# Reordering how an attention pair's q and k leave PSUM

## The chip, the cores and the metric

The kernel runs on one core of one Trainium2 chip. The metric is the device time of one execution in microseconds (us). The core has five engines that matter here: TensorE (PE, matrix multiplication; PEld is its weight load), ScalarE (ACT), VectorE (DVE), GpSimd (POOL) and SyncE (SP), which only issues DMAs. Each engine works through its own list of instructions in order and waits at an instruction until what it needs is there. TensorE writes its results into PSUM, eight banks of 128 partitions by 512 float32.

## The reference

Three transformer layers over 512 tokens of width 1024, float32. The first layer mixes block-sparse attention (8 heads of 64) with gated linear attention; the other two mix causal attention with a forget bias (8 heads of 64) with retention. Every layer ends in a feed-forward block of width 4096. What matters here is the attention, which the kernel computes for two heads at a time:

```python
scores = jnp.einsum('bqhd,bkhd->bhqk', q_i, k_i).astype(jnp.float32) * scale
logits = jnp.where(causal, scores + bias, -jnp.inf)
p = jax.nn.softmax(logits, axis=-1)
return jnp.einsum('bhqk,bkhd->bqhd', p.astype(v.dtype), v)
```

## The kernel before

`block1` is the first layer, `block2` runs twice. All large products are split into a high and a low part (`fp32r` tiles with names ending in h and l), three matmuls for each product. PSUM is two pools of four banks: `mm` for projections, `at` for attention and everything else that is short.

The order of work on TensorE is written out at build time by a planner, the class `Weave`. Each piece of the model is a generator; the planner keeps its own clock, books assumed costs on ScalarE, VectorE and GpSimd (`Engine`: ScalarE 0.2 + 0.83 per 1000 columns, VectorE 0.17 + 1.04, GpSimd 0.25 + 2.1), and resumes a generator when its event is due, the one with the lower priority number first. `wv.fork()` starts a new chain of bookings at the planner's present time, `wv.done()` gives an event that is due 0.6 (`LAG`) after the latest booking since the generator was resumed. A generator that yields `(1, ev)` asks for one free `at` bank and the event. The planner keeps an account of the `at` banks and none of the `mm` banks. The other engines' lists are ordered by a list scheduler in the framework: by program order, but an instruction that the scheduler believes ready may pass one that it believes is not. The framework adds the waits.

`attention_pair(i, ...)` handles heads 2i and 2i+1; there are four pairs in each of the three layers. It is given two PSUM banks, q and k, with head 0 on partitions 0 to 63 and head 1 on partitions 64 to 127. Its first loop makes three tiles for each head: `qs` (128 partitions: on the head's own half r the rounded q, on the other half x what rounding left), `kh` and `kl` (the high and the low part of k, each on both halves). In order, for each head:

- ScalarE writes `qs[r]` from the q bank; VectorE writes `qs[x]` from the q bank and `qs[r]`
- ScalarE writes `kh[r]` from the k bank; VectorE writes `kl[r]` from the k bank and `kh[r]` (`split2`)
- ScalarE copies `kh[r]` to `kh[x]`, then `kl[r]` to `kl[x]`
- `bias(2 * i + hh)` loads the head's bias row with a DMA on SyncE: `row` from `cd` in block2, where GpSimd then adds the causal mask (`cm`), or `g` from `revp` in block1

After that come the scores (TensorE, `at<-kh,qs` and `at<-kl,qs`), the masked minimum and the softmax (VectorE and ScalarE: `ea`, `eb`, `ec`, `mx`), transposes, copies (`pta`, `ptb`, `ptc`) and the product with v.

In block2 the q and k banks come from `proj_a`, so they are two of the four `mm` banks; pairs follow each other, and behind pair 3 stands `proj_b` for the retention values, which takes all four `mm` banks, one for each of four token tiles t = 0 to 3: t = 2 is given the bank of pair 3's q, t = 3 that of its k. In block1 transposes put q and k into two `at` banks.

Of the kernel before, what the change touches and what calls it, by code (L numbers as in the profile page):

```python
# [10 lines left out]
F32 = mybir.dt.float32  # L11
F32R = mybir.dt.float32r
I32 = mybir.dt.int32
AF = mybir.ActivationFunctionType
ALU = mybir.AluOpType
# [252 lines left out]
def model_kernel(ctx: ExitStack, tc: tile.TileContext, I, out):  # L268
# [13 lines left out]
    wv = Weave(8 - NM)  # L282
    act, dve, pool = Engine(nc.scalar, wv, 0.2, 0.83), Engine(nc.vector, wv, 0.17, 1.04), Engine(nc.gpsimd, wv, 0.25, 2.1)
    uid = [0]

    def nm(s):
        uid[0] += 1
        return f"{s}_{uid[0]}"

    def bt(s="b", dt=F32):  # L290
        return pb.tile([P, T], dt, tag="b", name=nm(s))
# [4 lines left out]
    def vt(s="v", w=16):  # L296
        if w > 16:
            return pv.tile([P, 40], F32, tag="w", name=nm(s), bufs=5)
        return pv.tile([P, 16], F32, tag="v", name=nm(s))
# [4 lines left out]
    def at_ps():  # L304
        t = psa.tile([P, T], F32, tag="at", name=nm("at"))
        wv.bank(t)
        return t

    def mm(out, lhsT, rhs, start, stop, more=False):

        nc.tensor.matmul(out, lhsT, rhs, start=start, stop=stop, skip_group_check=more)  # L311
        n = rhs.free_size()
        if lhsT.dtype == F32:
            c = max(4 * n, 1024 if n < P else 0) * (0.5 if lhsT.free_size() <= 64 else 1.0)
        else:
            c = n if n >= 256 else 4 * n
        wv.now += c / 2400.0

    def transpose(out, in_):
        nc.tensor.transpose(out, in_, ident)  # L320
        wv.now += 0.11

    def copy(o, i):
        act.activation(o, i, AF.Copy)

    def sub_lo(o, x, hi, eng=dve):
        eng.tensor_tensor(o, x, hi.bitcast(F32), ALU.subtract)

    def split2(hi, lo, x, scale=None):

        if scale is None:
            copy(hi, x)
            sub_lo(lo, x, hi)
        else:
            act.activation(hi, x, AF.Copy if isinstance(scale, float) else AF.Identity, scale=scale)
            dve.scalar_tensor_tensor(lo, x, scale, hi.bitcast(F32), ALU.mult, ALU.subtract)
# [170 lines left out]
    def attention_pair(i, operands, v, bias, acts_out, done=None):  # L507

        qps, kps, qscale, kscale = yield from operands()
        room, ops = [], []
        for hh in range(2):
            wv.fork()
            r, x = slice(64 * hh, 64 * hh + 64), slice(64 - 64 * hh, 128 - 64 * hh)
            sc = lambda c: c if c is None or isinstance(c, float) else c[r]
            qs, kh, klo = bt("qs", F32R), bt("kh", F32R), bt("kl", F32R)
            act.activation(qs[r], qps[r], AF.Copy if isinstance(qscale, float) else AF.Identity, scale=sc(qscale))
            dve.scalar_tensor_tensor(qs[x], qps[r], sc(qscale), qs[r].bitcast(F32), ALU.mult, ALU.subtract)  # L520
            split2(kh[r], klo[r], kps[r], sc(kscale))
            copy(kh[x], kh[r].bitcast(F32))
            copy(klo[x], klo[r].bitcast(F32))
            ops.append((qs, kh, klo, bias(2 * i + hh), wv.done()))
        ec, pc2 = bt("ec"), bt("ptc")
        for hh in range(2):
            qs, kh, kl, pieces, ev = ops[hh]

            ea, eb = bt("ea"), bt("eb")
            es = [eb[:, 384:512], ec[:, 256 * hh : 256 * hh + 256], eb[:, 0:384], ea]  # L530
            for t in (3, 2, 1, 0):
                if t:
                    yield 1, ev
                    sx = at_ps()
                    for u in (t, 0) if t == 1 else (t,):
                        m = max(P * u + P, 256)
                        s = sx[:, 256 * u : 256 * u + 256] if t == 1 else sx
                        mm(s[:, :m], qs[:, u * P : u * P + P], kh[:, :m], True, False)
                        mm(s[:, :m], qs[:, u * P : u * P + P], kl[:, :m], False, True)
                s = sx[:, 256 * t :] if t < 2 else sx  # L540
                wv.fork()
                e = es[t]
                mx = 3.0e38
                c = vt("mx")
                for j, (a, b, tl) in enumerate(pieces(t)):
                    dve.tensor_tensor_reduce(e[:, a:b], s[:, a:b], tl, 1.0, mx, ALU.add, ALU.min, c[:, j : j + 1])
                    mx = c[:, j : j + 1]
                act.activation(e, e, AF.Exp, bias=mx, scale=-1.0, accum_out=c[:, 2:3])
                dve.reciprocal(c[:, 3:4], c[:, 2:3])
                dve.tensor_scalar(e, e, c[:, 3:4], None, ALU.mult)  # L550
                if t == 3:
                    ev3 = wv.done()
            ev = wv.done()
            ev.t = max(ev.t, ev3.t)
            room.append((es, ev))

        pts = []
        for hh in range(2):
            es, t0 = room[hh]
            pta, ptb = bt("pta"), bt("ptb")  # L560
            pt = [pta, ptb[:, 0:384], pc2[:, 256 * hh : 256 * hh + 256], ptb[:, 384:512]]
            for ks, dst in (((0,), pta), ((1, 3), ptb), ((2,), pt[2])):
                yield 1, t0
                tp = at_ps()
                n = 0
                for kt in ks:
                    for t in range(kt, NT):
                        transpose(tp[:, n : n + P], es[t][:, kt * P : kt * P + P])
                        n += P
                if hh:  # L570
                    copy(dst, tp[:, 0:n])
                else:
                    dve.tensor_copy(dst, tp[:, 0:n])
            pts.append(pt)
        yield (1,)
        y = at_ps()
        for kt in range(NT):
            for hh in range(2):
                h = 2 * i + hh
                mm(  # L580
                    y[64 * hh : 64 * hh + 64, kt * P : T],
                    v[kt][:, 64 * h : 64 * h + 64],
                    pts[hh][kt],
                    kt == 0,
                    kt == NT - 1,
                )
        acts_out.split(i, y)
        if done is not None:
            wv.mark(done)
# [43 lines left out]
    class Quarter:  # L633
# [16 lines left out]
        def pieces(self, i, j):  # L650

            for k in range(2):
                k0 = self.k0 + 512 * i + 256 * k
                off, size = offs[(self.name, self.l, k0, k0 + 256, 512 * j, 512 * j + 512, "")]
                src = I["wall"][off : off + size].rearrange("(p w) -> p w", p=P)
                for c in range(2):
                    yield src[:, 512 * c : 512 * c + 512]
# [408 lines left out]
    def block1():  # L1066
# [32 lines left out]
        for i in range(4):  # L1099
            wv.spawn(attention_pair(i, operands(i), mv, moba_bias, ym, adone[i]), 1)  # L1100
# [160 lines left out]
    def block2(l, xw, h):  # L1261
# [11 lines left out]
        for i in range(4):  # L1273
            qk = []
            for j in range(2):
                qk.append((yield from proj_a("w_in_2", l, 512 * j + P * i, xw)))

            def operands(q, k):
                def get():
                    return q, k, -0.125, None  # L1280
                    yield

                return get

            wv.spawn(attention_pair(i, operands(*qk), fv, bias, mix), 1)
# [92 lines left out]
```

## Time and profile before

| | |
|---|---|
| median of 3 runs | 2027.2 us (2025.74 to 2028.43) |
| profiled execution | 2023.48 us |
| its span, first to last instruction | 2021.7 us |
| mean granted TensorE clock | 0.997 of full speed |

The profile is of one execution, some 3.7 us below the median. Times in it count from the start of the span. `L262` is the helper through which ScalarE, VectorE and GpSimd instructions are issued, `L311` the one for matmuls, so instructions are told apart by the tiles they write and read: `qs<-mm` writes a `qs` tile from an `mm` bank. A bracket behind a row gives the idle time of the engine just before it and what ended it.

### The profile page before, as it was taken

The page shows a single profiled execution, that of the slowest core. Times are in us where ns is not written, and L with a number is a line of the kernel's source. Part 1 is how long each engine was busy: PE and PEld are TensorE (multiplying, and loading weights), DVE is VectorE, ACT ScalarE, POOL GpSimd, SP SyncE. Part 2 cuts the span into 40 slices and gives each one's busy share as a digit, 9 for nine tenths or more (in the row PEclk, how much of TensorE's full clock was granted, in tenths as well). Part 3 has the DMA queues.
Part 4 walks back from the last instruction along what each step waited for, and adds up shares of the span by engine and source line. Part 5 has one row for each costly group of instructions (what it writes and reads, how often), then busy time and mean ns, then how long its engine had stood idle before and what let it go on. Part 6 is the DMA issues. An engine that isn't in the chain of part 4 may idle for free.

```text
span 2021.7 us, 25560 instructions
## 1 busy us (share of the span) xinstructions
PE 1986.7 (98%) x9574; PEld 1646.3 (81%) x9574; DVE 1165.7 (58%) x2052; ACT 936.4 (46%) x1639; POOL 281.8 (14%) x313
## 2 busy tenths in 40 slices
PE   8999999999999999999999999999999999999998
PEld 7777788888888888877888888888877889888886
DVE  6676444444556573475455656665575565656655
ACT  6566354333545453365332554552464324545550
POOL 2000110000212110010401201110111401211101
PEclk9999999999999999999999999999999999999999
DMA  6422123242766543332233745552422234655551
GB/s 202 157 90 78 53 65 103 94 146 74 187 162 133 155 125 115 100 106 88 78 126 111 158 138 134 148 148 81 132 94 84 73 115 146 135 156 156 131 142 42
DMA packets 93483, 240.50 MB, mean 119 GB/s; under 512 B 10734, under 2 KB 11200, under 8 KB 93360
## 3 DMA queue, kind: packets, MB, share of 16 engines
q1 hardware_dynamic: 72624, 201.12, 29.6%
q0 software_dynamic: 20736, 37.76, 11.5%
q8 instruction: 75, 1.23, 0.2%
q14 instruction: 48, 0.39, 0.1%
HBM read 236.69 MB, written 4.77 MB: 119 GB/s over the span
## 4 chain that ended last, share of the span: by engine, by line
PE 95%; DVE 2%; ACT 2%; issue 0%; POOL 0%; DMA 0%; POOLq 0%; DVEq 0%; SPq 0%; ACTq 0%
PE mm L311 67%; PE at L311 26%; PE at L320 2%; ACT wh L262 0%; DVE wl L262 0%; ACT kh L262 0%; ACT qs L262 0%; DVE og L262 0%; DVE h L262 0%; DVE qs L262 0%; POOL mv L262 0%; POOL gm L262 0%; ACT kl L262 0%; DMA xr<-in_xT_dram 0%; DVE cum L262 0%
## 5 line engine op out<-in xcount | busy, mean ns | idle before, releaser
L262 DVE TENSOR_TENSOR wl<-wr,wh 128x1024 fp32r<-128x1024 f32 (+1 forms) x265 | 334.9, 1266 | 316.7 <-ACT wh L262 315.1
L262 ACT ACTIVATE wh<-wr 128x1024 fp32r<-128x1024 f32 (+1 forms) x268 | 283.1, 1057 | 486.0 <-PE mm L311 346.4
L262 DVE TENSOR_TENSOR wl<-sw,wh 128x512 fp32r<-128x512 f32 x252 | 167.2, 688 | 179.1 <-ACT wh L262 178.9
L262 ACT ACTIVATE wh<-sw 128x512 fp32r<-128x512 f32 x252 | 151.2, 626 | 229.5 <-PE at L311 124.0
L311 PE MATMUL at<-hTh,wl 128*128 128x512 f32 (+1 forms) x640 | 242.2, 378 | 0.0
L311 PE MATMUL at<-hTh,wh 128*128 128x512 f32 (+1 forms) x640 | 242.2, 378 | 0.0
L311 PE MATMUL at<-hTl,wh 128*128 128x512 f32 (+1 forms) x640 | 242.2, 378 | 0.0
L311 PE MATMUL mm<-xTh,wh 128*128 128x512 f32 x536 | 213.9, 399 | 0.0
L669 POOL DMA_DIRECT2D sw<-in_wall_dram x144 | 126.6, 1016 | 600.2 <-DVE wl L262 504.6
L311 PE MATMUL mm<-xTl,wh 128*128 128x512 f32 x536 | 209.0, 390 | 0.0
L311 PE MATMUL mm<-xTh,wl 128*128 128x512 f32 x512 | 200.0, 391 | 0.0
L311 PE MATMUL mm<-wh,xl 128*128 128x512 f32 x504 | 196.1, 389 | 0.0
L311 PE MATMUL mm<-wl,xh 128*128 128x512 f32 x504 | 196.1, 389 | 0.0
L311 PE MATMUL mm<-wh,xh 128*128 128x512 f32 x504 | 196.1, 389 | 0.0
L311 PE MATMUL mm<-wh,xTh 128*128 128x512 f32 x352 | 144.5, 411 | 12.8 <-ACT wh L262 6.6
L311 PE MATMUL mm<-wl,xTh 128*128 128x512 f32 x352 | 139.0, 395 | 0.0
L311 PE MATMUL mm<-wh,xTl 128*128 128x512 f32 x352 | 138.9, 395 | 0.0
L311 PEld LDWEIGHTS at<-hTh,wl 128*128 128x128 f32 x640 | 120.4, 188 | 22.5
L311 PEld LDWEIGHTS at<-hTl,wh 128*128 128x128 f32 x640 | 120.4, 188 | 22.4
L311 PEld LDWEIGHTS at<-hTh,wh 128*128 128x128 f32 x640 | 120.4, 188 | 22.4
L311 PEld LDWEIGHTS mm<-xTh,wh 128*128 128x128 f32 x536 | 100.8, 188 | 19.6 <-ACT wh L262 0.5
L311 PEld LDWEIGHTS mm<-xTl,wh 128*128 128x128 f32 x536 | 100.9, 188 | 18.7
(283 smaller groups left out, 3705.1 us busy)
## 6 DMA issues: line engine op xcount, KB each, us to landing
wr<-in_wall_dram SPq DMA_DIRECT2D x266, 512.0 KB, 3.6
sw<-in_wall_dram SPq DMA_DIRECT2D x144, 256.0 KB, 5.7
sw<-in_wall_dram POOLq DMA_DIRECT2D x144, 256.0 KB, 6.0
row<-cd SPq DMA_DIRECT2D x16, 256.0 KB, 4.1
revp<-rev SPq DMA_DIRECT2D x1, 2560.0 KB
xr<-in_xT_dram SPq DMA_DIRECT2D x8, 256.0 KB, 6.1
g<-revp SPq DMA_DIRECT2D x8, 256.0 KB, 4.1
h<-in_x_dram SPq DMA_DIRECT2D x8, 256.0 KB, 5.7
```

The source lines that it names most:

```text
L262: return f(out, *a, **k)
L311: nc.tensor.matmul(out, lhsT, rhs, start=start, stop=stop, skip_group_check=more)
L320: nc.tensor.transpose(out, in_, ident)
L669: nc.gpsimd.dma_start(t, src, accum_op=ALU.add)
```

## The change

The one loop over the two heads becomes three. First both heads' q are read (ScalarE and VectorE), then both heads' k, and only then the copies to the other partitions, with each head's bias load and its event. The six tiles are asked for ahead of the loops. No instruction is added or taken away, and none changes its shape.

```diff
-        room, ops = [], []
+        room, ops, tiles = [], [], []
+
+        rows = [(slice(64 * hh, 64 * hh + 64), slice(64 - 64 * hh, 128 - 64 * hh)) for hh in range(2)]
+        for hh in range(2):
+            tiles.append((bt("qs", F32R), bt("kh", F32R), bt("kl", F32R)))
         for hh in range(2):
             wv.fork()
-            r, x = slice(64 * hh, 64 * hh + 64), slice(64 - 64 * hh, 128 - 64 * hh)
-            sc = lambda c: c if c is None or isinstance(c, float) else c[r]
-            qs, kh, klo = bt("qs", F32R), bt("kh", F32R), bt("kl", F32R)
-            act.activation(qs[r], qps[r], AF.Copy if isinstance(qscale, float) else AF.Identity, scale=sc(qscale))
-            dve.scalar_tensor_tensor(qs[x], qps[r], sc(qscale), qs[r].bitcast(F32), ALU.mult, ALU.subtract)
-            split2(kh[r], klo[r], kps[r], sc(kscale))
+            (r, x), qs = rows[hh], tiles[hh][0]
+            sc = qscale if isinstance(qscale, float) else qscale[r]
+            act.activation(qs[r], qps[r], AF.Copy if isinstance(qscale, float) else AF.Identity, scale=sc)
+            dve.scalar_tensor_tensor(qs[x], qps[r], sc, qs[r].bitcast(F32), ALU.mult, ALU.subtract)
+        for hh in range(2):
+            wv.fork()
+            (r, x), (_, kh, klo) = rows[hh], tiles[hh]
+            split2(kh[r], klo[r], kps[r], None if kscale is None else kscale[r])
+        for hh in range(2):
+            wv.fork()
+            (r, x), (qs, kh, klo) = rows[hh], tiles[hh]
             copy(kh[x], kh[r].bitcast(F32))
             copy(klo[x], klo[r].bitcast(F32))
             ops.append((qs, kh, klo, bias(2 * i + hh), wv.done()))
```

## Rows read from the trace of the kernel before

**Rows 1.** the page, part 1: each engine's busy time, share of the span, instructions

```profile
PE 1986.7 (98%) x9574; PEld 1646.3 (81%) x9574; DVE 1165.7 (58%) x2052; ACT 936.4 (46%) x1639; POOL 281.8 (14%) x313
```

**Rows 2.** busy time by stretch: length, then busy us of PE, PEld, DVE, ACT, POOL

```profile
80.00:270.00 190.00, 182.33 (x925) 145.37 (x924) 117.12 (x255) 104.05 (x207) 13.27 (x20) 0.99 0.27 89
870.00:1000.00 130.00, 126.12 (x660) 100.53 (x659) 80.76 (x259) 68.73 (x140) 29.49 (x26) 1.00 0.26 86
```

**Rows 3.** who waited for whom, TensorE: us in total, times, longest

```profile
PE mm L311 <- DVE qs L262: 5.9, 2, 2.9
PE at L311 <- DVE qs L262: 3.1, 2, 1.9
```

**Rows 4.** timeline of TensorE, pair 3 of the first block2 layer

```profile
909.54 0.40 PE L311 MATMUL mm<-wh,xTl 128*128 128x512 f32 x1
912.87 0.50 PE L311 MATMUL mm<-wh,xTh 128*128 128x512 f32 x1 [2.94 <-DVE qs L262]
...
914.59 0.39 PE L311 MATMUL mm<-wh,xTh 128*128 128x512 f32 x1
```

**Rows 5.** timeline of ScalarE there (start, duration, in brackets idle before)

```profile
907.66 0.57 ACT L262 ACTIVATE qs<-mm 64x512 fp32r<-64x512 f32 x1
...
910.86 0.63 ACT L262 ACTIVATE kl<-kl 64x512 fp32r<-64x512 f32 x1 [1.49 <-DVE kl L262]
911.50 0.59 ACT L262 ACTIVATE qs<-mm 64x512 fp32r<-64x512 f32 x1
```

**Rows 6.** timeline of VectorE there

```profile
909.43 0.68 DVE L262 SCALAR_TENSOR_TENSOR qs<-mm,qs 64x512 fp32r<-64x512 f32 x1
910.14 0.68 DVE L262 TENSOR_TENSOR kl<-mm,kh 64x512 fp32r<-64x512 f32 x1
912.12 0.69 DVE L262 SCALAR_TENSOR_TENSOR qs<-mm,qs 64x512 fp32r<-64x512 f32 x1 [1.30 <-ACT qs L262]
```

**Rows 7.** busy time of two like stretches, PEclk third from the right

```profile
1508.70:1516.54 7.84, 7.84 (x33) 6.27 (x34) 3.01 (x4) 3.41 (x6) 2.53 (x2) 0.78 0.01 3
912.87:919.17 6.30, 6.30 (x33) 5.18 (x34) 2.92 (x4) 3.41 (x6) 2.53 (x2) 1.00 0.02 9
```

**Rows 8.** timeline of three engines in block1, pairs 0 and 3

```profile
89.59 0.63 ACT L262 ACTIVATE kl<-kl 64x512 fp32r<-64x512 f32 x1 [0.90 <-DVE kl L262]
...
91.85 0.47 PE L311 MATMUL at<-g,u 96*128 96x512 f32 x1 [1.14 <-DVE qs L262]
...
102.72 0.44 PE L311 MATMUL at<-kh,qs 128*128 128x384 f32 x1 [1.56 <-DVE mx L262]
...
155.76 0.74 DVE L262 SCALAR_TENSOR_TENSOR qs<-at,gains,qs 64x512 fp32r<-64x512 f32 x1
...
156.73 0.68 ACT L262 ACTIVATE qs<-at,gains 64x512 fp32r<-64x512 f32 x1
...
158.34 0.36 PE L311 MATMUL at<-kh,qs 128*128 128x256 f32 x1 [1.94 <-DVE qs L262]
```

**Rows 9.** timeline of ScalarE and TensorE, block1, pair 1

```profile
125.14 0.61 ACT L262 ACTIVATE kl<-kl 64x512 fp32r<-64x512 f32 x1
...
127.81 0.39 PE L311 MATMUL at<-kh,qs 128*128 128x512 f32 x1
```

**Rows 10.** SyncE, VectorE, TensorE at pair 0 of block2; tile view of row

```profile
863.79 0.42 SPq L348 DMA_DIRECT2D row<-cd  x1
869.96 0.33 SPq L360 DMA_DIRECT2D wr<-in_wall_dram  x1
...
869.97 0.56 DVE L262 CUSTOM_DVE_ANT_0 ea<-at,row 128x384 f32<-128x384 f32 x1
...
872.36 0.33 PE L311 MATMUL at<-kh,qs 128*128 128x384 f32 x1
...
L262 POOL TENSOR_TENSOR cm<-row,tri x16: 1284/1292/1987, 863.0 to 1510.1; 128x512 f32<-128x512 f32 x16
...
DMA to landing us min/median/max: 3.7/4.4/6.8
```

## The prediction

> **What bounds the kernel now.** The first view is the page's table of engines: TensorE is busy 1986.7 of 2021.7 us, VectorE 58%, ScalarE 46% [rows 1]. All TensorE work stays, so the change can only reach the 35 us in which TensorE stands still, and the slowness of its clock. The second view is the busy time by stretch around the attention: TensorE is idle for 7.67 us between 80 and 270 (block1) and for 3.88 us of the 130 us around the pairs of the first block2 layer; the second has the same 3.88 [rows 2]. So 7.67 + 2 x 3.88 = 15.4 us is all that could be won from idle time near the pairs. The third view, TensorE's waits, names the part that belongs to the reordered instructions: 5.9 us in two waits for `qs` by a matmul into an `mm` bank, 3.1 us in two by one into an `at` bank [rows 3]. These are not waits for the operands; they are waits for a PSUM bank that the last reader of q has not left.
>
> The timelines of one such place show the chain. At pair 3 TensorE ends the second token tile of the value projection at 909.94, needs the bank of pair 3's q for the third, and starts again at 912.87, 2.94 us later [rows 4]. ScalarE read head 0's q at 907.66, then had k and a copy, then stood 1.49 us for VectorE's `kl` because the next thing in its list was the copy of `kl`; only at 911.50 did it read head 1's q [rows 5]. VectorE, free between 910.82 and 912.12, waited 1.30 us for that, and its read of head 1's q, 912.12 + 0.69 = 912.81, freed the bank [rows 6]. The copies that the change moves back are what stands between the two reads of q.
>
> **Part 1: the q bank in block2.** VectorE's first q read can't come sooner (it ends at 910.11, behind other work) [rows 6]. For what follows there are two bounds. If ScalarE may read head 1's half of the bank while VectorE reads head 0's, its read is done by about 909, and VectorE's second read is 910.14 to 910.82: the bank is free 912.81 - 910.82 = 1.99 us sooner. If the two engines take turns at a bank, ScalarE reads 910.13 to 910.72 (0.59, rows 5), VectorE does head 0's `kl` meanwhile, 910.14 to 910.82, and then q, to 911.52: 1.3 us sooner. Below, nothing: that would need the moved copies to stay in front, for which no row speaks. No row shows both engines in the two halves of one bank at once. The nearest is pair 3 of block1, where head 1's q read already stands ahead of the `kl` copy: ScalarE begins it at 156.73, after VectorE has ended head 0's at 156.50 [rows 8]. I take turns, 1.3 us, at two places (the second layer repeats the wait, longest 2.9, 5.9 in two [rows 3]): **2.6 us**, bounds 0 and 4.0.
>
> What is late next is pair 3's k bank, for the fourth token tile. TensorE wants it 914.59 - 912.87 = 1.72 us after it resumes [rows 4], so at 911.55 + 1.72 = 913.3. VectorE's last k read would be 911.55 to 912.23. It hides, with 1 us of cover; if it came no sooner than today (912.81 + 0.69 = 913.5) it would take back 0.2 us.
>
> The Trainium skill, "PSUM — Partial Sum Buffer", section "PSUM bank collisions raise a hardware error", has different 32-partition quadrants of one bank open to two engines at the same time and calls a guard by whole bank the simple version of the rule. The heads lie in different quadrants, so by that rule alone part 1 would be worth 2 x 1.99 = 4.0 us instead of 2.6; what decides is how coarsely this program is guarded, and the rows leave it open.
>
> **Part 2: block1.** At 91.85 TensorE waited 1.14 us for the `at` bank of pair 0's q, at 158.34 1.94 us for that of pair 3's [rows 8]. Pair 3's second q read on ScalarE, at 156.73, is already as early as turns allow, so I book nothing there; if both engines may read at once, VectorE's second read could follow its first, 156.50 to 157.24 plus some 0.1, where TensorE today starts at 158.34: bound 1.0. At pair 0 ScalarE's stall of 0.90 us for `kl` goes [rows 8]; it stands in a chain through ScalarE and VectorE that ends in the wait of 1.56 us at 102.72 [rows 8]. The 1.14 us wait may stay, because the planner counts these banks and will itself ask sooner. I take **0.8 us**, most of the 0.90; bounds 0 and 1.14 + 1.56 = 2.7.
>
> **Part 3: the clock.** After the 2.94 us wait in the second block2 layer TensorE ran at half its clock (1.2 instead of 2.4 GHz) for a while: the same 33 matmuls took 7.84 us there at a mean of 0.78 and 6.30 in the first layer at 1.00 [rows 7]. The same idle time brought the low clock once in two. Cut from 2.94 to 1.6 us, it is less likely to bring it: the waits of 1.56 and 1.94 in block1 are of that size [rows 8], though the mean clock of that stretch is 0.99 [rows 2], so a spell of the low clock came there too, without so long a wait. I book the spell gone: 7.84 - 6.30 = **1.54 us**; bounds 0 and 3.1 (both layers, in executions that have it in both).
>
> **Part 4: what is moved and could cost.** Head 0's operands are ready later: two ScalarE reads of head 1, 0.59 each [rows 5], now stand before its copies, 1.2 us. The planner doesn't know it. In its bookings for block2 head 0's event was due after q and k in turn on ScalarE and VectorE (0.625 + 0.70, twice), two copies (0.625 each), the mask on GpSimd (1.325) and `LAG`, 5.83 in all; now six ScalarE instructions follow each other without a gap, 3.75 + 1.325 + 0.6 = 5.68. Head 1's goes from 8.41 to 5.075 + 1.325 + 0.6 = 7.00. Cover: the shortest lead that I found is pair 1 of block1, last copy ended 125.75, first score matmul 127.81, 2.06 us [rows 9]. 1.2 is less than 2.06, so I cost it at nothing; with the lead gone it would be up to 1.2 us a pair. Head 1's scores are planned 1.4 us sooner, filler matmuls move behind them, and TensorE's list changes a little all through the attention; no row prices that, and the bounds are a wait like the smaller ones seen, 1.5 us [rows 8], gained or lost in each of three layers: 4.5 either way. Nothing says which, so 0.
>
> The bias loads move too: two DMAs for each pair in SyncE's queue, now behind both heads' k, and in block2 two mask additions on GpSimd (1.29 us each [rows 10]). At pair 0 the second load is issued at 863.79; the first, today one weight load sooner, would join it. 863.79 + 4.4 + 1.29 = 869.5, and VectorE first uses the row at 869.97 [rows 10]: hidden by 0.5 us, and the row itself by 1.8.
>
> **Sum.** 2.6 + 0.8 + 1.5 = 4.9 us. The profiled execution would go from 2023.48 to 2018.6; it lies 3.7 below the median of the runs, so the median goes from 2027.2 to **2022.3**. One can tell some 0.2%, 4.05 us, from no change here: below 2023.15 is faster, above 2031.25 slower.
>
> **The rivals.**
> *Both halves at once.* 4.0 + 1.0 + 0.8 + 1.5 = 7.3, so 2019.9. For it: the heads' partitions are apart, and no instruction of the other head needs the first one's result. Against it: 156.73 behind 156.50 [rows 8], which may be chance. (The page named in part 1 would allow it.)
> *The half clock stays* or comes at another idle spot: 3.4 us, 2023.8, no measurable change. For it: block1's spell without a wait of 2.9 us ahead of it. Against it: in block2 the longest idle time is nearly halved.
> *The change doesn't do what it says*: TensorE's new order puts a wait elsewhere as large as what it saves, for a bank that it now asks for sooner; 2027.2, within 2 us. For it: every event of the planner shifts. Against it: it keeps no account of `mm` banks, so the two large waits are not of its making.
> *Slower: the bias row of pair 0 falls behind one more weight load*, the one that SyncE issues at 869.96 [rows 10]. Then the row lands at 870.3 + 4.4 = 874.7 and the mask is added by 876.0; the first score bank is released about then and TensorE, which wants it at 872.36 [rows 10], waits 3.7 us, in two layers 7.4, and each such wait is longer than the one that the half clock followed [rows 7], 1.54 each. 2.6 + 0.8 + 1.5 saved, 7.4 + 3.1 lost: +5.6, 2032.8. It decides as soon as the load is issued after 869.97 - 4.4 = 865.6. Against it: the row has only to stay ahead of one weight load, and there are 6 us between the two.
>
> **How the numbers follow.** Forecast 0.42 (own range 2020 to 2024.5, of it 0.36 faster), both halves 0.14, clock stays 0.18 (0.03 of it faster), no effect 0.15, slower 0.11. Faster: 0.36 + 0.14 + 0.03 = 0.53; same: 0.06 + 0.15 + 0.15 = 0.36; slower 0.11. The range runs from both halves with a second half-clock spell gone (2019.9 - 1.5 = 2018.4) to no effect and a little over, 2028.2; outside lie the slower case and some of the tails.
>
> **What would show it.** In the timelines of pair 3, ScalarE's second `qs` read follows the first without a `kl` copy between, and starts just as VectorE's first ends (turns) or before it (both halves). TensorE's two waits for `qs` shrink from 2.94 to 1.6 or 0.9 us. ScalarE's waits for `kl` fall away. The clock after pair 3 is 1.00 in both layers. Wrong would be: the same wait for `kl` or `qs`, a new wait of TensorE for `mx`, `row` or `cm`, or a bias load behind the next weight load.

## The result and the profile after

The change made the kernel slower. In five runs each, the changed kernel took 2038.77 us (median; 2037.14 to 2040.54) and the kernel before 2025.74 us (2025.24 to 2028.43): ratio 1.0064, 95% interval 1.0053 to 1.0075, some 13 us. (The forecast counted from 2027.2, the median of three of these runs of the kernel before.) The profiled execution took 2040.54 us, 17.1 more than that of before, with a span of 2038.8 us and a mean granted clock of 0.993.

The page's table of engines, beside [rows 1]. The work is the same; PE is "busy" 6 us longer, much as the lower clock in the next view would have it:

```profile
PE 1992.8 (98%) x9574; PEld 1651.1 (81%) x9574; DVE 1164.4 (57%) x2052; ACT 938.2 (46%) x1639; POOL 283.4 (14%) x313
```

Busy time of the stretches of [rows 2], then of four shorter ones that begin where a stall of TensorE ends. In the stretch of block1 PE is busy 7.6 us less than before, in block2's 1.0 less; three of the four stalls are followed by a low clock (0.52 is about 1.2 GHz throughout, 0.77 for about half of the stretch), the fourth, a short one, is not:

```profile
80.00:270.00 190.00, 174.73 (x863) 138.76 (x862) 112.23 (x248) 102.78 (x204) 10.55 (x16) 0.96 0.25 87
870.00:1000.00 130.00, 125.13 (x633) 99.59 (x632) 79.36 (x248) 71.02 (x144) 24.44 (x20) 0.99 0.28 90
...
98.42:105.50 7.08, 6.68 (x16) 4.78 (x17) 3.67 (x6) 6.80 (x12) 0.00 (x0) 0.52 0.29 112
153.42:160.50 7.08, 7.08 (x27) 6.09 (x28) 6.89 (x34) 5.68 (x19) 0.00 (x0) 0.77 0.19 69
900.63:904.20 3.57, 3.57 (x11) 2.99 (x12) 0.78 (x2) 0.60 (x1) 0.00 (x0) 0.52 0.43 147
929.04:935.34 6.30, 6.30 (x29) 4.92 (x31) 2.40 (x3) 4.59 (x8) 2.54 (x2) 1.00 0.23 76
```

TensorE's waits, beside [rows 3]. The two waits for `qs` by a matmul into an `mm` bank went from 5.9 us to 1.6, as forecast or better. Above them stand three that have grown (before: 1.7, 1.6 and 3.1 us):

```profile
PE at L320 <- DVE pta L262: 5.9, 2, 2.9
PE at L311 <- DVE mx L262: 5.8, 1, 5.8
PE at L311 <- DVE qs L262: 5.2, 2, 4.8
...
PE mm L311 <- DVE qs L262: 1.6, 2, 0.8
```

The place that the prediction was made from, pair 3 of the first block2 layer, on ScalarE, VectorE and TensorE, beside [rows 4 to 6]. The second `qs` read follows the first, and starts as VectorE's first ends:

```profile
926.24 0.58 ACT L262 ACTIVATE qs<-mm 64x512 fp32r<-64x512 f32 x1
927.57 0.59 ACT L262 ACTIVATE qs<-mm 64x512 fp32r<-64x512 f32 x1 [0.75 <-DVE qs L262]
...
926.86 0.68 DVE L262 SCALAR_TENSOR_TENSOR qs<-mm,qs 64x512 fp32r<-64x512 f32 x1 [0.79 <-ACT qs L262]
...
929.04 0.47 PE L311 MATMUL mm<-wh,xTh 128*128 128x512 f32 x1 [0.80 <-DVE qs L262]
```

Where the time went is at pair 0 of block1, beside [rows 8]. On ScalarE a weight copy, `wh`, stands in front of the first `qs` read; it sat there for 5.44 us and began when TensorE had ended the last matmul that it could run (93.20 + 0.39). VectorE's `wl` stands in front of its own `qs` read and waited with it. TensorE, whose transposes of q and k had been done since 88.4, then stood 4.83 us for the bank:

```profile
93.68 1.06 ACT L262 ACTIVATE wh<-wr 128x1024 fp32r<-128x1024 f32 x1 [5.44 <-issue]
94.76 0.68 ACT L262 ACTIVATE qs<-at,gains 64x512 fp32r<-64x512 f32 x1
96.80 0.68 ACT L262 ACTIVATE qs<-at,gains 64x512 fp32r<-64x512 f32 x1 [1.36 <-DVE qs L262]
...
94.77 1.23 DVE L262 TENSOR_TENSOR wl<-wr,wh 128x1024 fp32r<-128x1024 f32 x1 [5.26 <-ACT wh L262]
96.03 0.74 DVE L262 SCALAR_TENSOR_TENSOR qs<-at,gains,qs 64x512 fp32r<-64x512 f32 x1
...
93.20 0.39 PE L311 MATMUL mm<-wh,xTl 128*128 128x512 f32 x1
98.42 0.61 PE L311 MATMUL at<-g,u 96*128 96x512 f32 x1 [4.83 <-DVE qs L262]
```

In block2 the picture repeats on VectorE. `wl` stands in front of the copy `pta`, which empties a bank that TensorE filled by 897.7; `wl` waits for ScalarE's `wh`, and `wh` stands behind the copies to the other partitions, the last three of which now follow each other:

```profile
896.80 0.61 ACT L262 ACTIVATE kl<-kl 64x512 fp32r<-64x512 f32 x1
897.44 1.06 ACT L262 ACTIVATE wh<-wr 128x1024 fp32r<-128x1024 f32 x1
...
898.53 1.23 DVE L262 TENSOR_TENSOR wl<-wr,wh 128x1024 fp32r<-128x1024 f32 x1 [2.08 <-ACT wh L262]
899.79 0.69 DVE L262 COPY pta<-at 128x512 f32<-128x512 f32 x1
...
900.63 0.37 PE L320 MATMUL at<-ident,ec 128*128 128x128 f32 x1 [2.93 <-DVE pta L262]
```

The third stall, 5.81 us for `mx` at 153.42, is at pair 2 of block1, whose operands TensorE's new list puts right behind pair 1's. VectorE came to the minimum that empties the score bank by way of `qd`, for which it waited 1.72 us on ScalarE, `ki`, a `wl` that took 2.09 us, and `gqk`. The weight copy is 2.26 us of this stall (2.09 and 0.17 of waiting), not the whole of it:

```profile
148.48 0.69 DVE L262 SCALAR_TENSOR_TENSOR qd<-gqk,qd 128x512 f32<-128x512 f32 x1 [1.72 <-ACT qd L262]
...
149.94 2.09 DVE L262 TENSOR_TENSOR wl<-wr,wh 128x1024 fp32r<-128x1024 f32 x1 [0.17 <-ACT wh L262]
152.07 0.69 DVE L262 TENSOR_TENSOR gqk<-mm,rb 128x512 f32<-128x512 f32 x1
152.67 0.68 DVE L262 CUSTOM_DVE_ANT_0 ea<-at,g 128x512 f32<-128x512 f32 x1
```

By the starts of the weight copies, which both kernels have in the same number, 11.8 of the 17.1 us came in block1's attention (from 1.5 us behind at 86 us to 13.3 at 167), some 2.3 and 1.1 at the pairs of the two block2 layers (13.9 to 16.2, then 16.0 to 17.1), and 1.5 before any attention ran; the little that is left lies between them.

### The profile page after: what moved, and what is told of

Read it like the earlier page. It is cut to its first block, busy times and chain, and to the rows that moved or that the text cites. A ratio compares the mean times of both kernels' runs of the same rounds, so it can differ in the third digit from the quotient of the medians.

```text
span 2038.8 us, 25556 instructions
## 1 busy us (share of the span) xinstructions
PE 1992.8 (98%) x9574; PEld 1651.1 (81%) x9574; DVE 1164.4 (57%) x2052; ACT 938.2 (46%) x1639; POOL 283.4 (14%) x313
```

## The experiments

### Is it TensorE's list or the order of the reads?

The change does two things at once: the reads run in another order, and the planner, which books them, writes another list for TensorE. The two can be taken apart, since the bookings can be made in one order and the instructions issued in the other. With the old bookings TensorE's list is, instruction for instruction, that of before; with the new ones, that of the changed kernel (in the traces all 9574 matmuls follow each other in the same order of tiles and shapes).

```diff
+        def read(ps):
+            wv.charge(act, 0.2 + 0.83 * 0.512, (ps,))
+            wv.charge(dve, 0.17 + 1.04 * 0.512, (ps,))
...
+        for hh in range(2):
+            wv.fork()
+            read(qps)
+            read(kps)
+            spread()
+        keep = wv.chain, wv.ready, dict(wv.banks), [list(e.busy) for e in (act, dve, pool)]
...
+        wv.chain, wv.ready, wv.banks = keep[:3]
+        for e, b in zip((act, dve, pool), keep[3]):
+            e.busy = b
+        ops = [(*o[:4], ev) for o, ev in zip(ops, evs)]
```

`spread` books the two copies and the mask, and makes the event. The instructions are issued between `keep` and the lines that put the bookings back. *New order, old list:*

> The instructions are issued in the new order, but the planner books them, and makes the two heads' events due, as in the old order; so TensorE's list is instruction for instruction that of the kernel before. Theory P (the loss comes from TensorE's list, which the planner wrote anew because the bookings moved, and from what the other engines' lists become with it): 3 to 5 us faster than before, 0.9975 to 0.9985 of it, with the two waits for qs in block2 at 1.6 us or less and no wait of 4.8 us for qs or 5.8 us for mx in block1. Theory R (the new order of the reads costs by itself: taking turns at a bank holds both heads back): 9 to 13 us slower than before, with TensorE waiting for qs or mx in block1 as in the changed kernel.

2033.59 us against 2025.36, ratio 1.0041 (1.0029 to 1.0054). Both theories missed: the wait for `qs` went from 2.94 to 1.64 us in each layer, exactly the 1.3 of theory P, and the kernel is 8 us slower all the same; its profiled execution lost some 5 us in block1 and 2 to 3 in each block2 layer. Its TensorE, VectorE and ScalarE at pair 3 of block2:

```profile
917.62 0.50 PE L311 MATMUL mm<-wh,xTh 128*128 128x512 f32 x1 [1.64 <-DVE qs L262]
919.77 0.47 PE L311 MATMUL mm<-wh,xTh 128*128 128x512 f32 x1 [0.28 <-DVE kl L262]
925.07 0.30 PE L320 MATMUL at<-ident,eb 128*128 128x128 f32 x1 [2.08 <-DVE ptb L262]
...
922.97 1.23 DVE L262 TENSOR_TENSOR wl<-wr,wh 128x1024 fp32r<-128x1024 f32 x1 [3.35 <-ACT wh L262]
924.23 0.69 DVE L262 COPY ptb<-at 128x512 f32<-128x512 f32 x1
...
921.88 1.06 ACT L262 ACTIVATE wh<-wr 128x1024 fp32r<-128x1024 f32 x1 [1.29 <-PE mm L311]
```

Again a `wl` stands in front of a bank's copy, waits for `wh`, and `wh` waits for a matmul of TensorE, that is for one of the six weight slots. In the kernel before the two instructions of VectorE stand the other way round, and `wl` waits just as long at nobody's cost:

```profile
913.58 0.69 DVE L262 COPY ptb<-at 128x512 f32<-128x512 f32 x1
...
917.72 1.23 DVE L262 TENSOR_TENSOR wl<-wr,wh 128x1024 fp32r<-128x1024 f32 x1 [3.12 <-ACT wh L262]
```

The same kernel under another label, which speaks of a rule for the weight copies that the kernel doesn't have, repeated time and waits (2034.14 us, one run):

> The new order of the instructions with the old bookings once more, for one more look at its profile: 2033 to 2036, TensorE waiting 2.08 us for ptb in each block2 layer, with VectorE's weight copy wl standing in front of that copy and waiting for ScalarE's wh.

*Old order, new list:*

> The reverse: the instructions are issued in the old order, but the planner books them as in the new one; TensorE's list is that of the changed kernel. Theory P: 13 to 18 us slower than before (the changed kernel's loss of 13 and what the new order of the reads saves, 2.6 to 5), with the long waits of the changed kernel in block1. Theory R: within 3 us of before.

2036.36 us, ratio 1.0053 (1.004 to 1.0066): 11 us slower, a little under theory P's band, with the long waits of block1. In block2 TensorE's list did no net harm here: by the starts of the weight copies the kernel is 10.2 us behind at 244 us and 10.6 at its end, with waits for `qs` of 1.06 and 0.88 us in place of 2.94 and new ones for `eb` of 2.00 and 2.28.

```profile
98.23 0.77 PE L311 MATMUL at<-g,u 96*128 96x512 f32 x1 [6.24 <-DVE qs L262]
...
149.96 0.44 PE L311 MATMUL at<-kh,qs 128*128 128x384 f32 x1 [4.07 <-DVE mx L262]
```

So each half alone costs 8 to 11 us, and both together 13: the costs do not add up. Neither "the list" nor "the reads" alone explains it. What the long stalls have in common is a weight copy in front of the instruction that frees the bank.

### Where is it?

Each block's lists change for themselves, so the change can be made in one of them (`if not isinstance(qscale, float)` picks block1).

> The change in block1's four pairs alone. By the starts of the weight copies, which come in the same number in both kernels, the changed kernel lies 1.5 us behind before at 86 us of its span and 13.3 behind from 165 us on: so 11 to 14 us slower than before under either theory, if block1 makes the loss alone. If the two blocks' lists work on each other (one long chain of small shifts, theory C), anything from 0 to 17 slower.

2037.33 us, ratio 1.0058 (1.0045 to 1.007): 12 us, as read from the weight copies.

> The change in block2's eight pairs alone (two layers). By the same starts of weight copies the changed kernel loses 2.2 us more at the first layer's pairs and 1.0 at the second's: 2 to 4 us slower than before, although the waits for qs shrink by 2 us in each layer; TensorE's new wait of 2.9 us for pta stays and a spell of half clock after it. My prediction's parts 1 and 3 alone would make it 4 us faster.

2027.82 us, ratio 1.0017 (1.0008 to 1.0026): 2.5 to 3.5 us slower, with `qs` down from 5.9 to 1.6 us and `pta`, 5.9, in its place. In this stretch, too, a saving of 4.3 us was given back with interest.

### Weight copies behind the reads

Theory W: the stalls come from weight copies that the framework's scheduler puts in front of instructions which free a PSUM bank. A weight block is asked for, in program order, just before its first matmul; the scheduler takes its copies forward, and what it passes there are the pairs' bank reads. How far it takes them in the planner's time no trace shows, and the 35 us below is a setting of the test. The test keeps the chosen TensorE list and queues a block's copies behind those bank reads of a pair that were planned more than 35 us before the block's first use (the last eight of them on each engine):

```diff
+LEAD = 35
...
+            if tn(out).startswith(PAIR) and any(tn(x).startswith(("at_", "mm_")) for x in a):
+                self.reads.append((self.wv.now, ins.ins))
...
+    def behind(eng):
+        stack = ExitStack()
+        for ins in [i for t, i in eng.reads if t < wv.now - LEAD][-8:]:
+            stack.enter_context(tc.issue_after(ins))
+        return stack
...
-            copy(hi[:, c], raw[:, c])
+            with behind(act):
+                copy(hi[:, c], raw[:, c])
...
-            sub_lo(lo[:, c], raw[:, c], hi[:, c])
+            with behind(dve):
+                sub_lo(lo[:, c], raw[:, c], hi[:, c])
```

> The changed kernel with one rule added: a weight block's two copies (wh on ScalarE, wl on VectorE) are queued behind those instructions of an attention pair that read a PSUM bank and that the planner placed more than 35 us before the block's first use. TensorE's list is that of the changed kernel. Theory W (the loss is weight copies that the scheduler now puts in front of instructions which free a bank: wh and wl in front of pair 0's q reads in block1, wl in front of the copy pta in block2, wl in front of the minimum of pair 2): the waits of 4.8 us for qs and twice 2.9 us for pta fall below 1 us, and the half clock behind them goes with them; 9 to 16 us less than the changed kernel, so 2023 to 2030, ratio to before 0.999 to 1.0025. Theory T (the reads and copies in their new order are late by themselves, taking turns at a bank, and whatever stands beside them does not matter): within 3 us of the changed kernel, 1.005 to 1.008.

2023.17 us against 2026.11, ratio 0.9987 (0.9978 to 0.9995). The same instructions with the same TensorE list went from 13 us slower to 3 us faster than before, at the top of theory W's band. TensorE's waits: `pta` and the long `qs` are gone, the two for pair 3's q stay at 0.80. The one for `mx` is down from 5.81 to 3.55, by 2.26 us, and that is just what the weight copy had in that stall: no `wl` stands between `ki` and `gqk` now (VectorE, then TensorE):

```profile
140.84 0.68 DVE L265 TENSOR_TENSOR ki<-gqk,ki 128x512 f32<-128x512 f32 x1
141.55 0.69 DVE L265 TENSOR_TENSOR gqk<-mm,rb 128x512 f32<-128x512 f32 x1
...
142.90 0.44 PE L318 MATMUL at<-kh,qs 128*128 128x384 f32 x1 [3.55 <-DVE mx L265]
```

> Control: the kernel before with the same rule. Theory W: before has no long wait behind a weight copy, so the rule gains little, 0 to 4 us (0.998 to 1.000); the waits of 2.94 us for qs stay within 1.2 us of what they were. If the rule by itself is worth as much as in the changed kernel (9 us or more), theory W explains the kernel's slowness but not the change's.

2023.43 us, ratio 0.9988 (0.9979 to 0.9997): the rule is worth 2.4 us to the kernel before and 15.6 to the changed one (0.0077 of 2026). Theory W holds for the loss, and theory T, by which it doesn't matter what stands beside the reads, falls.

*One block's copies alone.* In the next kernel only the two copies in front of pair 0's q are held back, behind the two heads' q reads (`eng.reads[:2]`, `PAIR = ("qs_",)`).

> The changed kernel, in which one weight block's two copies (wh on ScalarE, wl on VectorE), those that stand in front of pair 0's q reads in block1, are queued behind the two heads' q reads. Theory W (a weight copy in front of a read that frees a bank makes the loss): the wait of 4.83 us for qs falls below 1 us and the half clock behind it goes, 5 to 8 us less than the changed kernel, 2031 to 2034, while the waits of 5.8 us for mx and twice 2.9 us for pta stay. Theory S (any shift of the lists rearranges everything, and no single copy matters): within 3 us of the changed kernel, or a gain with those later waits changed too.

2035.53 us, ratio 1.0041 (1.0028 to 1.0053), 4.7 us less than the changed kernel (0.0023 of 2026). It fell just short of the band, and the trace says why: the copy went back by three places only, and now stands between the two heads' k reads, so that a wait of 2.51 us for `kl` took the place of the 4.83, and a low clock followed again (a mean of 0.76 from 96.41 to 103.49). The waits for `mx` (5.83) and `pta` (2.93, twice) did not move, against theory S. ScalarE, then TensorE:

```profile
90.41 0.68 ACT L265 ACTIVATE kh<-at,gains 64x512 fp32r<-64x512 f32 x1
93.05 1.06 ACT L265 ACTIVATE wh<-wr 128x1024 fp32r<-128x1024 f32 x1 [1.95 <-issue]
...
96.41 0.47 PE L318 MATMUL at<-g,u 96*128 96x512 f32 x1 [2.51 <-DVE kl L265]
```

> The changed kernel with the rule of the run before last (a weight block's copies behind bank reads of a pair planned more than 35 us before the block's first use) in block2's two layers alone; block1 is that of the changed kernel. Theory W: the two waits of 2.93 us for pta fall below 1 us, with the half clock behind them; 5 to 9 us less than the changed kernel, 2030 to 2034. Theory S: within 3 us of it.

2030.67 us, ratio 1.0022 (1.0013 to 1.0031): 8.5 us less than the changed kernel; the waits for `pta` are gone, and those of block1 stay. With the 4.7 of the one copy in block1 that is 13.2 of the 15.6.

### What the reordered reads are worth with the rule in place

> The instructions in the new order, the planner's bookings and TensorE's list as in the kernel before, and the rule for the weight copies. Theory W: the waits of 2.08 us for ptb go; what remains of the change is what my prediction's part 1 named, the wait for pair 3's q bank, 2.00 in the kernel before with the rule, and 1.3 less here in each layer: 2019 to 2024. Theory T (the new order of the reads costs by itself): 2028 to 2034, since without the rule it was 8 us slower than before.

2020.77 us, ratio 0.9971 (0.996 to 0.9983): 5 to 6 us faster than before, and some 14 less than without the rule (0.0070 of 2026). At pair 3 of block2 the wait for q's bank, 2.00 us with the rule and the old order, is 0.70, and that for k's 0.27; the `ptb` waits are gone. The first fence is the kernel before with the rule, the second this one:

```profile
914.95 0.49 PE L318 MATMUL mm<-wh,xTh 128*128 128x512 f32 x1 [2.00 <-DVE qs L265]
```

```profile
160.86 0.47 PE L318 MATMUL at<-kh,qs 128*128 128x256 f32 x1 [3.24 <-DVE qs L265]
...
913.49 0.50 PE L318 MATMUL mm<-wh,xTh 128*128 128x512 f32 x1 [0.70 <-DVE qs L265]
915.65 0.47 PE L318 MATMUL mm<-wh,xTh 128*128 128x512 f32 x1 [0.27 <-DVE kl L265]
```

> The fourth corner: the instructions in the old order, the planner's bookings and TensorE's list as in the changed kernel, and the rule for the weight copies at 35 us. Without the rule it was 11 us slower than before. Theory W: most of that was weight copies in front of bank reads, so 5 to 12 us less than without the rule, 2024 to 2031; the wait for mx in block1, which every kernel with the changed kernel's TensorE list has shown, stays at 3.5 us or more. If TensorE's list by itself makes the loss, it stays within 3 us of 2036.

2020.24 us, ratio 0.9971 (0.9959 to 0.9983), 16 us less than without the rule; better than either theory's band. Its wait for `mx` is still 3.01 us (expected: 3.5 or more) and its waits for `qs` in block2 2.15, and it is as fast as any.

The four corners follow. Each ratio is against the kernel before as timed on the same chip; the last two columns, of one profiled execution each, are the start in us of TensorE's first matmul on `hTh`, which comes behind block1's attention. Kernels with the same block1 differ there by up to 1.2 us (487.0 and 486.8; 500.3, 499.9 and 499.1).

| instructions | TensorE's list | without the rule | with the rule | block1 without | block1 with |
|---|---|---|---|---|---|
| old order | old | 1 | 0.9988 (0.9979 to 0.9997) | 487.0 | 491.3 |
| new order | old | 1.0041 (1.0029 to 1.0054) | 0.9971 (0.9960 to 0.9983) | 492.4 | 491.1 |
| old order | new | 1.0053 (1.0040 to 1.0066) | 0.9971 (0.9959 to 0.9983) | 497.1 | 488.4 |
| new order | new | 1.0064 (1.0053 to 1.0075) | 0.9987 (0.9978 to 0.9995) | 500.3 | 490.2 |

With the rule the four lie within 0.17% of each other, with intervals that overlap: the losses of the left column go with the places of the weight copies. The change as a whole, last row against first, is then worth nothing that these runs can tell (2023.17 against 2023.43 us).

The rule doesn't clear the way everywhere, so its column is not the worth of order and list with nothing in front. In block1 it gives back 1.3 of the 5.4 us that the new order with the old list loses, and it costs the kernel before 4.3: it moves a weight copy that ScalarE began at 148.16 to 154.46, just in front of pair 3's q reads, and TensorE's wait there grows from 1.94 to 4.59 us. The 3.24 above is of the same kind (`wl` at 157.03, VectorE's first `qs` read at 158.47). In the kernel before with the rule:

```profile
155.54 1.32 DVE L265 TENSOR_TENSOR wl<-wr,wh 128x1024 fp32r<-128x1024 f32 x1 [0.16 <-ACT wh L265]
...
160.72 0.36 PE L318 MATMUL at<-kh,qs 128*128 128x256 f32 x1 [4.59 <-DVE qs L265]
```

### Holding them back further

> The changed kernel with the rule at 20 us in place of 35: weight copies are held back further. If the last large wait (3.55 us for mx in block1, behind another weight copy) is of the same kind, it goes: 2016 to 2022. If the copies now come too late, TensorE waits for wh or wl in the attention, and it is 2024 or more.

2025.9 us, ratio 0.9996 (0.9987 to 1.0005). Both expectations missed in part. The 3.55 us for `mx` were not behind a weight copy, as the lines of the kernel with the rule at 35 show, so they couldn't go. Held back further, a `wl` stands there again, and the wait is back at 5.83. So 2.3 us of that wait are a weight copy's, and 3.55 stay without one. With the old order of the reads and the new list the wait is 3.01, and no kernel with the old list has one for `mx` above 1.6: that part comes with TensorE's new list. And TensorE did not wait for weights but for other work that came later, a copy of v and the `og` of the linear attention (VectorE, then TensorE):

```profile
142.70 2.10 DVE L265 TENSOR_TENSOR wl<-wr,wh 128x1024 fp32r<-128x1024 f32 x1 [0.17 <-ACT wh L265]
...
108.91 0.50 PE L318 MATMUL mm<-xTh,wh 128*128 128x512 f32 x1 [2.33 <-ACT v L265]
146.19 0.69 PE L318 MATMUL at<-kh,qs 128*128 128x384 f32 x1 [5.83 <-DVE mx L265]
...
224.48 1.56 PE L327 MATMUL at<-ident,og 128*128 128x128 f32 x4 [4.45 <-DVE og L265]
```

## Why the prediction was wrong

The forecast was 2022.3 us, and the changed kernel took 2038.8. The step that failed is part 4, its second half: "TensorE's list changes a little all through the attention; no row prices that, and the bounds are a wait like the smaller ones seen, 1.5 us [rows 8], gained or lost in each of three layers: 4.5 either way. Nothing says which, so 0." It went wrong twice.

**It looked at one list of three.** ScalarE's and VectorE's lists are written anew as well, by a scheduler that believes some instructions ready, and among those that it moves are copies of 1024 columns that must wait for a weight slot. The prediction checked what the moved instructions had in front of them in the old lists, and not what could come to stand in front of them in new ones. The rows to see it by were there: TensorE's idle time depends on which short copy stands behind which `wl`, and VectorE's waits for `wh` (one of 3.12 us right behind pair 3, above) are longer than the bound of 1.5 us that was taken. TensorE's own list is not free of blame: 3.0 to 3.55 us of the wait for `mx` came with it, where pair 2's operands now follow right behind pair 1's.

**It sized the bound by the smaller waits.** The stalls with a weight copy in front of the read or copy that frees a bank lasted 2.1 to 6.2 us, and a lower clock followed most of them. In the 7.08 us after 98.42 TensorE was busy for 6.68 at 0.52, so some 3.2 us of them went to the clock (6.68 x 0.48). Pinning the weight copies gave back 15.6 us, where the bound was 4.5.

The other steps:

- *Part 1 was right for the q bank, and to the tenth.* ScalarE and VectorE take turns at a bank: the second `qs` read waited 0.75 and 1.36 us for VectorE's first in the rows shown. With the old TensorE list the wait fell by 2.94 - 1.64 = 1.30 us, and with the rule by 2.00 - 0.70 = 1.30, at two places each. As a time, the kernel before with the rule takes 1530.4 us from the first matmul on `hTh` to the end of its span, the new order with the old list and the rule 1527.3: 3.1 us, near the 2.6 (one execution each; the whole kernels' intervals overlap). The k bank was taken for hidden with 1 us of cover, and TensorE waits 0.27 for it: the reads of k take turns as well, so with the old list the last of them ended 2.06 us after the last of q (919.62 and 917.56), where the prediction had 0.71. The quadrant rule of the Trainium skill, "PSUM — Partial Sum Buffer", section "PSUM bank collisions raise a hardware error", does not describe how this program is guarded: in none of the 14 traces do the two engines' reads of a pair's q bank overlap, and the rival "both halves at once" falls.
- *Part 2* (0.8 us in block1) did not come. With the new order and the old list, pair 0's waits were 0.35 and 1.06 us in place of 1.14 and 1.56, but two of 0.5 for `z` came between them, and in front of the wait for pair 3's q, whose 1.94 stayed at 1.75, came two of 0.81 and 0.88.
- *Part 3* fits, and was overtaken: no low clock follows the short wait of 0.80 us (1.00 after 929.04), but the new stalls brought more of it than was saved. The length of the wait alone doesn't tell: in the kernel before with the rule the same wait of 2.00 us was followed by a mean clock of 0.73 in the first layer (914.95 to 921.25) and of 1.00 in the second.
- *Part 4, the rest:* TensorE did not wait for a bias row or mask in any run, so the rival on the slower side named the right sign by the wrong mechanism; that is luck. Head 0's later operands, costed at nothing, made one wait of 0.28 us with the new order and the old list, at pair 1 of block1 for ScalarE's `kl`. TensorE's other waits for `kl` there (0.27 to 0.81 us) end with VectorE's last read of a k bank.
- *The rival "the change doesn't do what it says"* came nearest, a new wait elsewhere "as large as what it saves"; it had the place in part wrong (TensorE's list rather than all three) and the size by a factor of three or more.

What stays open: why the scheduler takes a given weight copy past a given read when bookings or order shift, since its beliefs leave no record in a trace; what the 3.55 us for `mx` without a weight copy are made of, beyond VectorE's wait of 1.72 us for ScalarE's `qd`; what order and list are worth with no weight copy in front of any bank read, which no run isolates; and whether order and list together are worth 0.1% less than either alone, or the same.

## What to carry to other kernels

Where a scheduler orders an engine's list, an edit's price is not only in the instructions that it moves: ask which long instruction with a wait of its own could come to stand in front of a short one that frees a buffer, and take that one's wait, with the low clock that may follow it, as the bound. A reordering that is measured as a loss may be harmless, or a good one, with an accident: pin the accident (here, weight copies behind the reads of banks) and measure again, and do so to the kernel before as well. Look then for the accidents that the pin itself makes, like the 4.59 us above. With the rule, either half of the change ran 0.3% below the kernel before, and both together 0.1%, which is what the rule alone does.

## What the runs showed of the hardware

VectorE's `wl` took 2.09 us at 149.94 in the changed kernel and 2.02 in the one with the old order and the new list, where the mean of all 263 is 1266 ns. In both, GpSimd began a product of two tiles, `kd`, within 0.1 us of it (at 149.91 in the first). The Trainium skill, "SBUF — State Buffer", section "SBUF: two separate sides", has the two engines share a pair of ports that one of them holds for a whole instruction. By that, an estimate, 1.04 us of waiting and 1.27 of work make 2.3; the row shows a little less, 2.09. Eight more `wl` of the changed kernel, from 335.54 on, took 2.28 us each, and each began 0.1 us after a GpSimd product `z` of 1.29 to 1.30. GpSimd's row for the first:

```profile
149.91 1.04 POOL L262 TENSOR_TENSOR kd<-ki,el 128x512 f32<-128x512 f32 x1 [99.99 <-issue]
```

The group of all `wl` of the changed kernel: busy us and mean ns, then the idle time before them and what ended it:

```profile
L262 DVE TENSOR_TENSOR wl<-wr,wh 128x1024 fp32r<-128x1024 f32 x263 | 332.2, 1266 | 334.6 <-ACT wh L262 333.5
```
